# A new order of the engine queues in the gated unit of an S5 layer

## The chip, the cores and the metric

The kernel runs on one core of one Trainium2 chip. A core has five engines with a queue each, worked off strictly in order: TensorE (PE in the profile; its weight loads are PEld), VectorE (DVE), ScalarE (ACT), GpSimd (POOL) and SyncE (SP, which here only issues DMAs). Engines wait for one another through semaphores. The metric is the device time of one execution in microseconds (us), given as the median of several runs.

## The reference, cut to what matters

One layer of a diffusion backbone on 1024 latent tokens of width 1024, with a context prefix of 256 tokens: a bidirectional S5 scan, then a gated unit, then a SwiGLU feed-forward part and a last RMS norm. The part around the change:

```python
g = gelu(y)                                   # y: output of the scan, 1024 x 1024
y = g * sigmoid(g @ w_glu + b_glu)            # the gated unit
x = x + gate * y                              # residual
h = modulate(rms_norm(x, norm_ffn), shift, scale)
x = x + gate2 * ((silu(h @ w1) * (h @ w3)) @ w2)   # 2816 hidden units
return rms_norm(x, norm_final)
```

## The kernel before, in words

Everything is fp32. A matmul operand is split into a high part (a copy rounded to `fp32r`) and a low part (the operand minus its high part), and each product is made of three matmuls, high by high, high by low and low by high.

The 1024 x 1024 x 1024 product `g @ w_glu` is made by a seven-product scheme (`ORDER`, line 1156): seven products of 512 x 512 x 512, whose left operands are blocks, sums and differences of blocks of the weight (L11, L12, S2, S3, L22, S1, S4) and whose right operands are blocks and differences of the activations (R11, R21, T2, T3, T4, T1, R22). The differences T are taken by VectorE, the sums S by DMAs that accumulate.

The order of everything in this unit is written out by hand, as one string of words, `TODO` (line 1157). A loop (`for word in TODO.split(): todo(word)`, line 1371) issues the instructions of one word after the other, so that each engine's queue holds its instructions in the order in which the words stand; the words of different engines are tied only by semaphores. Most words have the form `name:index:...`, and where the engine can be chosen the last letter names it (`D` or `V` VectorE, `P` or `E` GpSimd, `A` ScalarE). The words are (names of `todo`, lines 1232 to 1350):

- `.` or a number: one step, or so many, of TensorE. A step is three matmuls of 128x512 for one k of 4 of one column block q of 4 of one product p: step 16p + 4q + k + 1. Products 0 to 6 are the seven; steps 113 to 128 are the first 16 of the feed-forward part (line 1205). Each block (p, q) gathers in one of five PSUM banks used in rotation, except that product 1 adds into the banks of product 0. So the first step of a block waits until the block five before it has been read for the last time.
- `gT:k:j`, `bT:k:j`: four TensorE transposes (a quad) into one of two further banks; `gA` is the GELU from it (ScalarE), `bC` a copy from it, `bQ` a squared copy from it (ScalarE) and `bR` its sum (VectorE).
- `Rh`, `Rl`, `Wh`, `Wl`: high and low part of a right operand (128x512) or of a half of a left operand (128x1024). The copies are ScalarE's, `Wl` is always GpSimd's, `Rl` is VectorE's (`D`) or GpSimd's (`P`).
- `m`, `t2`, `t3`, `t4`: the differences, on VectorE, from SBUF to SBUF. `s`, `f`, `h`: accumulating DMAs issued from GpSimd's queue (they make S2, S4 and S1). `l`, `x`, `Q`, `R`: loads issued from SyncE's queue (`x:2` the third piece of the residual stream).
- `p` copies a first product's bank to SBUF (ScalarE). `u`, `v`, `c`, `d1`, `d2`, `E1` combine the products' banks (VectorE, one operand in PSUM). Then, for each of the 16 output blocks in the families e, c, d and E, `eS` is the sigmoid (ScalarE), `eM` multiplies by the gate column and by g (VectorE, one operand in PSUM) and `eX` adds the residual. With the letter `s`, `eM` writes to SBUF and frees the bank, and `eX` is GpSimd's; without, `eX` is VectorE's, reads PSUM, and frees the bank.
- `q`: a squared sum (ScalarE). `z:j`: 14 instructions of VectorE, 13 of them 128x4 and nine of those with two SBUF inputs, that make 1/rms of token half j and copy it out to 128x512; `Z:j`: eight TensorE matmuls that spread it over the rows. `hT` (VectorE, one operand in PSUM) applies it; `hH`, or `hI` and `hC`, makes the high part (ScalarE) and `hL` the low part, on VectorE (`V`) or GpSimd (`E`). `hT` writes one of three buffers in rotation.
- `oh`, `ol`: high and low part of the first feed-forward weights (ScalarE, GpSimd). `L:g`, `L:h`, `L:l`: gate, high and low part of the first rows of `w2`. `S:0`, `M:0`, `G:0`: SiLU, product and split of the feed-forward part's first tile.

After the string, `up_plain(0, 1, rest)` (line 1407) goes on with 16 more steps, the matmuls `pu` of the profile, in banks of a new PSUM pool; it needs the first four `hH` and `hL` of token half 1. All later stages are bound to TensorE's queue in the same way.

Two instructions of helpers carry most of the rows: line 78 is every `tensor_tensor`, line 81 every `scalar_tensor_tensor`, on VectorE or GpSimd. In the rows, `pp` are the five rotating banks, `pq` the two banks of the quads, `prb` the bank of `Z`; `c`, `rr`, `ru`, `rxa`, `rxc`, `rw` and `r` lie in SBUF. The step's lines:

```python
if k == 0:
    ZT.append(ZT[q] if p == 1 else pp())
(lh, ll), (rh, rl) = (SL[x] for x in ORDER[p])
cs_, z = slice(P * q, P * q + P), ZT[4 * p + q]
for n, (w, b) in enumerate(((lh, rh), (lh, rl), (ll, rh))):
    PE.matmul(z, w[:, k, cs_], b[:, k], start=p != 1 and k + n == 0, ...)
```

Of the kernel before, what the change touches and what calls it, by code (L numbers as in the profile page):

```python
# [1872 lines left out]
```

## Time and profile before

| | us |
|---|---|
| median of 3 runs | 1033.13 |
| lowest and highest run | 1031.77, 1033.31 |
| the profiled execution's own time | 1031.7 |
| its span | 1029.9 |
| TensorE, VectorE, ScalarE, GpSimd busy over the span | 957.5, 820.9, 450.3, 773.7 |
| the unit, from its first quad (267.35 us) to the first `pu` matmul (390.37 us) | 123.0 |

Start times in the rows are counted from the start of the span. A row of the timeline gives start, duration, engine, line, operation, output<-inputs, shape, how many like instructions are merged in it, and in square brackets the idle time of the engine ahead of it with the instruction that ended it. Neighbouring instructions of one engine overlap in the records by about 0.1 us, so that the cost of one in a row of many is the distance of the starts.

### The profile page before, as it was taken

How to read it: one execution, taken by the hardware profiler on the slowest of the kernel's cores; microseconds unless marked ns; L12 is line 12 of the kernel's file. 1: busy time of each engine (PE TensorE's matmuls, PEld its weight loads, DVE VectorE, ACT ScalarE, POOL GpSimd, SP SyncE). 2: the span in 40 equal slices, each digit the busy share in tenths (PEclk: the TensorE clock that was granted, in tenths of full speed). 3: DMA queues.
4: the chain of work that ended last, by engine and by line, in shares of the span. 5: the costliest groups of instructions: out<-in, count | busy, mean ns of one | idle time of the engine just before them, and what ended most of it. 6: DMA issues, size and time to landing. Idle time of an engine off the chain costs nothing. (4 is left out here: it accounts for less than half of the span.)

```text
span 1029.9 us, 17603 instructions
## 1 busy us (share of the span) xinstructions
PE 957.5 (93%) x6572; PEld 750.8 (73%) x6572; DVE 820.9 (80%) x1580; ACT 450.3 (44%) x827; POOL 773.7 (75%) x595
## 2 busy tenths in 40 slices
PE   5988798878998798999999999999999999999996
PEld 1466523667877676888888888888888888888885
DVE  7979799995589889788877768695968768586977
ACT  4468622323554675534334332434334343424337
POOL 5799899991578355888787777778687877778674
PEclk9989999989999899999999999999999999999998
DMA  9764997213944211011211112121212011121204
GB/s 322 284 136 92 286 349 230 89 52 93 238 102 135 91 42 61 21 41 41 82 42 43 50 46 68 52 71 42 83 41 71 29 55 62 42 72 52 72 21 164
DMA packets 50793, 102.04 MB, mean 99 GB/s; under 512 B 4490, under 2 KB 19082, under 8 KB 49684
## 3 DMA queue, kind: packets, MB, share of 16 engines
q1 hardware_dynamic: 44372, 85.60, 25.2%
q0 software_dynamic: 3168, 11.54, 5.9%
q10 hardware_dynamic: 3168, 3.79, 1.1%
q8 instruction: 52, 0.85, 0.3%
q14 instruction: 33, 0.27, 0.1%
HBM read 85.30 MB, written 6.16 MB: 89 GB/s over the span
## 5 line engine op out<-in xcount | busy, mean ns | idle before, releaser
L78 POOL TENSOR_TENSOR rr<-rxc,rr 128x512 fp32r<-128x512 f32 (+1 forms) x130 | 172.6, 1341 | 63.1 <-ACT rr L1187 56.2
L1358 PE MATMUL ut<-rr,rr 128*128 128x512 f32 x400 | 155.7, 389 | 0.2 <-POOL rr L78 0.2
L1356 PE MATMUL ut<-rr,rr 128*128 128x512 f32 x400 | 155.6, 389 | 0.0
L1187 ACT CAST rr<-rxc 128x512 fp32r<-128x512 f32 x124 | 76.9, 622 | 148.3 <-PE xt L1680 51.5
L1680 PE MATMUL xt<-rr,c 128*128 128x512 f32 x540 | 129.7, 389 | 0.0
L1357 PE MATMUL ut<-c,rr 128*128 128x512 f32 x320 | 124.5, 389 | 0.0
L1680 PEld LDWEIGHTS xt<-rr,c 128*128 128x128 f32 x540 | 101.4, 188 | 21.0
L78 DVE TENSOR_TENSOR ru<-ru,xt 128x1024 f32<-128x1024 f32 x90 | 106.7, 1212 | 8.1 <-PE xt L1680 6.3
L78 DVE TENSOR_TENSOR ru<-ut,ru 128x512 f32<-128x512 f32 x98 | 67.1, 686 | 42.0 <-PE ut L1358 36.5
L1357 PE MATMUL ut<-rr,rr 128*128 128x512 f32 x240 | 93.4, 389 | 0.0
L1358 PEld LDWEIGHTS ut<-rr,rr 128*128 128x128 f32 x400 | 75.1, 188 | 16.3 <-POOL rr L78 0.6
L1356 PEld LDWEIGHTS ut<-rr,rr 128*128 128x128 f32 x400 | 75.1, 188 | 15.6
L1357 PEld LDWEIGHTS ut<-c,rr 128*128 128x128 f32 x320 | 60.1, 188 | 12.4
L78 POOL TENSOR_TENSOR rr<-rw,rr 128x512 fp32r<-128x512 f32 x27 | 37.7, 1396 | 37.8 <-ACT rr L1187 37.8
L78 POOL TENSOR_TENSOR rr<-ru,rr 128x512 fp32r<-128x512 f32 (+1 forms) x40 | 58.7, 1468 | 9.5 <-ACT rr L1187 5.7
L1356 PE MATMUL ut<-c,rr 128*128 128x512 f32 x160 | 62.3, 389 | 0.1
L1358 PE MATMUL ut<-c,rr 128*128 128x512 f32 x160 | 62.2, 389 | 0.0
L78 POOL TENSOR_TENSOR rxc<-rxc 128x512 f32<-128x512 f32 x40 | 60.6, 1516 | 1.6
L1680 PE MATMUL ut<-rr,c 128*128 128x512 f32 x216 | 51.9, 389 | 0.0
L1357 PEld LDWEIGHTS ut<-rr,rr 128*128 128x128 f32 x240 | 45.0, 188 | 9.3
L586 PE MATMUL pv<-ru,c 128*64 128x160 f32 x512 | 45.5, 316 | 5.2 <-ACT ru L499 2.0
L1218 PE MATMUL pp<-rr,rr 128*128 128x512 f32 x192 | 48.1, 407 | 1.9 <-DVE rr L78 1.9
(460 smaller groups left out, 2427.5 us busy)
## 6 DMA issues: line engine op xcount, KB each, us to landing
c<-in_ada_w SPq DMA_DIRECT2D x46, 256.0 KB, 5.5
rxc<-in_w SPq DMA_DIRECT2D x38, 256.0 KB
rxc<-in_w SPq DMA_DIRECT2D x19, 512.0 KB, 3.6
rw<-in_w SPq DMA_DIRECT2D x11, 512.0 KB
ru<-in_w SPq DMA_DIRECT2D x11, 512.0 KB
ra<-in_ada_w SPq DMA_DIRECT2D x10, 512.0 KB, 10.7
ra<-in_ada_w SPq DMA_DIRECT2D x18, 256.0 KB, 6.0
ru<-in_xT SPq DMA_DIRECT2D x4, 1024.0 KB
```

What stands on the lines that cost most here:

```text
L78: eng.tensor_tensor(out=o, in0=x, in1=y, op=op)
L586: PE.matmul(pv[64 * (i % 2):64 * (i % 2) + 64, ri, c0:c0 + 160], w[:, i, 64 * ri:64 * ri + 64], U[:, 8 * b + 4 * j + i], start=True, stop= ...
L1187: S.copy(o[0], x)
L1218: PE.matmul(z, w[:, k, cs_], b[:, k], start=p != 1 and k + n == 0, stop=k == 3 and n == 2, skip_group_check=p == 1)
L1356: PE.matmul(pu, wh, bh, start=start, stop=False)
L1357: PE.matmul(pu, wh, bl, start=False, stop=False)
L1358: PE.matmul(pu, wl, bh, start=False, stop=stop)
L1680: PE.matmul(pd, w[:, cs_], b, start=j in (1, 2, 4) and n == 0, stop=n == 2, skip_group_check=j not in (1, 2, 4))
```

## The change

The string `TODO` is replaced by another. It holds the same work: 128 steps, 26 quads, and the same words, apart from the engine of some: of the `Rl`, R21:2, R22:0, T1:2 and T2:3 go from GpSimd to VectorE and T1:0, T3:2 and T4:3 from VectorE to GpSimd; of the `eM`/`eX` pairs, e:1, e:3, c:0 and E:0 become VectorE's and c:1, c:2, c:3, E:1 and E:3 GpSimd's; of the `hL`, 0:0 and 1:5 go to VectorE and 0:3, 0:5, 1:0 and 1:6 to GpSimd (with `hI` and `hC` in the place of `hH`, or the other way round); of the `bC`, 0:0 and 7:1 go to ScalarE, 0:1, 4:0, 5:1 and 6:0 to VectorE. Otherwise only the order of the words differs, and with it the order of each engine's queue. No other line is changed.

```diff
--- before.py
+++ after.py
@@ -1154,27 +1154,27 @@
 
 
         ORDER = (("L11", "R11"), ("L12", "R21"), ("S2", "T2"), ("S3", "T3"), ("L22", "T4"), ("S1", "T1"), ("S4", "R22"))
-        TODO = """gT:6:0 x:0 . Wh:L12:1 . Rh:R21:0 Wl:L12:1 gT:7:0 Rh:R21:1 . gA:6:0 . gA:7:0 Wh:L12:0 gT:1:1 Rl:R21:0:D s:0 gT:4:1 . Rh:R21:3
-            Rl:R21:1:D gA:4:1 . Wl:L12:0 gA:1:1 . Rh:R21:2 gT:3:1 gT:0:1 gA:3:1 . Rl:R21:3:D s:1 p:0 . m:3 gA:0:1 p:1 . Rl:R21:2:P . t3:0
-            gT:2:1 gT:7:1 m:1 gA:2:1 . m:0 gA:7:1 . m:2 p:2 . t3:3 Rh:T3:0 gT:6:1 t2:0 Wh:S3:0 gT:5:1 Rl:T3:0:D . gA:5:1 t2:3 f:0 . Wh:S2:0
-            t3:1 . t2:1 Rh:T2:3 . Wl:S2:0 p:3 . Rh:T3:1 Rh:T2:0 . gA:6:1 . Rh:T2:1 f:1 Rl:T3:1:D . Wh:S2:1 t3:2 . Rl:T2:3:P Wh:S3:1 2 Rh:T3:2
-            l:0 t2:2 eS:e:0 . Wl:S2:1 2 Rh:T2:2 eM:e:0 . Rh:T3:3 Rl:T2:0:D eS:e:1 . Rl:T2:2:P eX:e:0:D eS:e:2 l:1 . eM:e:1:s . Rl:T2:1:P eM:e:2
-            . eS:e:3 eX:e:2:D bT:0:0 Wh:L22:0 Wl:S3:1 eM:e:3:s 3 Wh:L22:1 . t4:2 Q:2 . u:0 Wl:L22:0 Rh:T4:2 3 Rl:T3:2:D h:0 . Rl:T3:3:D .
-            eX:e:3:P u:1 2 Rl:T4:2:D Wl:S3:0 u:2 . Rh:T1:0 . Rh:T1:1 . Rh:T1:2 bT:2:0 Rh:T1:3 t4:1 . u:3 Rl:T1:2:P Wh:S1:0 2 Rh:T4:1 t4:0 .
-            bC:2:0:A eX:e:1:P Rh:T4:0 . v:0 . Rl:T4:1:D x:1 . Rl:T4:0:P . t4:3 . Wl:L22:1 v:1 . Rh:T4:3 3 Rl:T4:3:D h:1 . Rl:T1:3:D Rh:R22:0
-            x:2 . v:2 Wl:S1:0 Wh:S4:0 . Rh:R22:2 . v:3 Wh:S4:1 . Rl:T1:0:D Q:0 Rh:R22:1 . Rl:R22:0:P bC:0:0:D Rh:R22:3 2 Rl:T1:1:D . c:0
-            Wl:S4:0 Wh:S1:1 bT:1:0 . eS:c:0 bC:1:0:D . eM:c:0:s Rl:R22:3:P . c:1 . eS:c:1 Rl:R22:1:D . Wl:S1:1 eM:c:1 . eX:c:1:D . c:2 . eS:c:2
-            bT:5:0 Wl:S4:1 Q:1 bT:3:0 eM:c:2 bC:5:0:A . bC:3:0:A eX:c:2:D . q:0:0:0 . Rl:R22:2:P c:3 q:0:0:1 R:0 bT:6:0 . eS:c:3 eX:c:0:P
-            q:0:0:2 . eM:c:3 bC:6:0:A . eX:c:3:D q:0:0:3 bT:4:0 L:g x:3 bT:7:0 bC:4:0:A . bC:7:0:A d1:0 . q:1:0:0 d2:0 . q:1:0:1 . eS:d:0 .
-            d1:1 q:1:0:2 . eM:d:0:s q:1:0:3 . d2:1 eX:d:0:P . z:0 eS:d:1 2 oh:0:0 . oh:0:2 ol:0:0 d1:2 bT:4:1 oh:0:3 Z:0 eM:d:1:s bC:4:1:A
-            ol:0:2 d2:2 oh:0:1 . hT:0:0 . eS:d:2 eX:d:1:P d1:3 . hI:0:0 eM:d:2:s hC:0:0 . ol:0:1 hT:0:1 bT:5:1 . d2:3 eX:d:2:P hH:0:1 hT:0:2 .
-            bC:5:1:A eS:d:3 E1:0 . hL:0:0:E hI:0:2 eM:d:3:s bT:6:1 eS:E:0 . hL:0:1:V hC:0:2 . bC:6:1:A eX:d:3:P hT:0:3 . eM:E:0:s hH:0:3 .
-            hL:0:2:E E1:1 . hT:0:4 eS:E:1 eX:E:0:P bT:7:1 hT:0:5 hH:0:4 . bC:7:1:D hH:0:5 . ol:0:3 E1:2 q:1:1:0 . eM:E:1 eS:E:2 . R:1 hL:0:5:V
-            q:1:1:1 bT:0:1 eX:E:1:D L:h . hL:0:3:V . q:1:1:2 eM:E:2 L:l . bC:0:1:A hT:0:6 . q:1:1:3 eX:E:2:D . hI:0:6 E1:3 bQ:0:1 bT:2:1
-            hL:0:4:V hC:0:6 bT:1:1 bR:0:1 eS:E:3 . hL:0:6:E hT:0:7 bC:2:1:A . bQ:1:1 eM:E:3 hI:0:7 bR:1:1 . bC:1:1:A eX:E:3:D bQ:2:1 hC:0:7
-            bR:2:1 bT:3:1 hL:0:7:E bC:3:1:A bQ:3:1 bR:3:1 . z:1 . S:0 3 Z:1 . hT:1:0 . hT:1:2 hH:1:0 . hT:1:1 hH:1:2 . hL:1:0:V hI:1:1 hL:1:2:V
-            hC:1:1 hT:1:3 hL:1:1:E hT:1:5 hH:1:3 M:0 hI:1:5 hL:1:3:V G:0:h hT:1:4 hC:1:5 hT:1:6 hL:1:5:E hH:1:4 hH:1:6 hL:1:4:V hT:1:7 hH:1:7
-            hL:1:6:V hL:1:7:V G:0:l"""
+        TODO = """. x:0 s:0 Rh:R21:0 gT:2:1 Wh:L12:0 gT:4:1 Rl:R21:0:D . gA:4:1 Wl:L12:0 . gA:2:1 . Rh:R21:1 Wh:L12:1 gT:7:1 gT:0:1 . gA:7:1 s:1
+            Rl:R21:1:D gA:0:1 m:2 gT:6:0 p:0 gT:5:1 Wl:L12:1 gA:6:0 . gA:5:1 . Rh:R21:2 . Wh:S2:0 f:0 gT:3:1 m:0 gT:7:0 Rl:R21:2:D . gA:3:1
+            Wl:S2:0 gA:7:0 . Rh:R21:3 . Wh:S2:1 . f:1 . t2:0 p:2 Rl:R21:3:D . Rh:T2:0 Wl:S2:1 . Wh:S3:0 l:0 . gT:1:1 Wh:S3:1 . Wl:S3:0 . p:1
+            p:3 . gA:1:1 . l:1 . Wl:S3:1 3 t3:0 Q:2 . m:1 Rh:T3:0 . t2:1 gT:6:1 m:3 Rh:T2:1 . t2:3 gA:6:1 . Rl:T2:1:P Rh:T2:3 . eS:e:0 . t2:2 .
+            t3:2 . Rh:T2:2 Rl:T2:0:D Wh:L22:0 Rl:T2:3:D . Rl:T2:2:P eM:e:0 . eS:e:3 eX:e:0:D Rh:T3:2 Wl:L22:0 eS:e:1 eM:e:3 . Wh:L22:1 eM:e:1 2
+            eS:e:2 eX:e:1:D . eM:e:2 Wl:L22:1 . eX:e:2:D . u:0 eX:e:3:D . Rl:T3:2:P u:1 . x:1 . h:0 t4:2 bT:3:0 t3:1 . Rh:T4:2 h:1 Rl:T3:0:D
+            Rh:T3:1 . t3:3 . Rh:T1:0 Rl:T3:1:D . Rh:T3:3 u:2 Rl:T1:0:P Rh:T1:1 . Rh:T1:2 . Rl:T1:1:D Rh:T1:3 . Rl:T1:2:D . Rl:T1:3:D t4:0
+            bT:0:0 bC:3:0:A Rl:T4:2:D bC:0:0:A bT:2:0 Rl:T3:3:D Rh:T4:0 bT:1:0 bC:2:0:A u:3 Rl:T4:0:P . Wh:S1:0 bC:1:0:D . v:0 Wh:S1:1 .
+            Wl:S1:0 . q:0:0:0 . q:0:0:1 . v:1 Wl:S1:1 q:0:0:2 Q:0 . q:0:0:3 3 t4:1 Q:1 v:2 . Rh:T4:1 t4:3 Rh:R22:0 . Rl:T4:1:D Rh:T4:3 .
+            Rl:R22:0:D Rh:R22:1 . Rl:T4:3:P v:3 Wh:S4:1 . Rh:R22:2 . Wl:S4:1 x:2 Rh:R22:3 . Wh:S4:0 . c:0 . eS:c:0 Rl:R22:2:P . eM:c:0 .
+            Wl:S4:0 . c:1 . eS:c:1 . eX:c:0:D . Rl:R22:3:P R:0 eM:c:1:s . c:2 eX:c:1:P . eS:c:2 . Rl:R22:1:D . eM:c:2:s . c:3 eX:c:2:P bT:5:0
+            bT:4:0 bC:5:0:A . bC:4:0:D eS:c:3 . eM:c:3:s . L:g 2 eX:c:3:P d1:0 bT:6:0 d2:0 . bC:6:0:D x:3 eS:d:0 . eM:d:0:s bT:7:0 . d1:1
+            eX:d:0:P bC:7:0:A . d2:1 q:1:0:0 . q:1:0:1 . q:1:0:2 . d1:2 q:1:0:3 . d2:2 oh:0:0 . z:0 eS:d:2 . ol:0:0 oh:0:3 . oh:0:2 ol:0:3
+            bT:4:1 oh:0:1 . bC:4:1:A eM:d:2:s . ol:0:1 eS:d:1 d1:3 Z:0 d2:3 eX:d:2:P . hT:0:2 eS:d:3 . eM:d:3:s ol:0:2 hI:0:2 bT:6:1 hT:0:0
+            hC:0:2 . bC:6:1:A eX:d:3:P E1:0 R:1 . hH:0:0 eM:d:1:s . eS:E:0 hL:0:2:E hT:0:1 . E1:1 hH:0:1 bT:7:1 eX:d:1:P hT:0:5 . eS:E:1
+            bC:7:1:A eM:E:0 . hI:0:5 hL:0:0:V . hC:0:5 hT:0:3 bT:5:1 hL:0:5:E . bC:5:1:D hI:0:3 . eM:E:1:s hC:0:3 . q:1:1:0 E1:2 eX:E:1:P .
+            eX:E:0:D eS:E:2 . L:h hL:0:3:E E1:3 bT:0:1 eM:E:2 eS:E:3 bT:1:1 L:l q:1:1:1 hT:0:6 eM:E:3:s q:1:1:2 eX:E:2:D q:1:1:3 bC:0:1:D
+            eX:E:3:P bQ:0:1 hI:0:6 bT:2:1 bR:0:1 hC:0:6 bC:2:1:A hL:0:1:V bQ:1:1 hL:0:6:E hT:0:4 . bC:1:1:A . hH:0:4 bR:1:1 . hL:0:4:V bQ:2:1
+            bT:3:1 . bR:2:1 bC:3:1:A hT:0:7 . bQ:3:1 . hI:0:7 bR:3:1 hC:0:7 z:1 hL:0:7:E . Z:1 S:0 . hT:1:2 . hT:1:0 hH:1:2 . hT:1:1 hI:1:0 .
+            hL:1:2:V hC:1:0 . hI:1:1 hT:1:5 hL:1:0:E . hC:1:1 hH:1:5 . hL:1:1:E hT:1:3 . hH:1:3 hT:1:4 hL:1:3:V hH:1:4 hT:1:6 hL:1:4:V hI:1:6
+            hL:1:5:V hC:1:6 hT:1:7 hL:1:6:E M:0 hH:1:7 G:0:h hL:1:7:V G:0:l"""
         WS = dict(L12=wb, S2=wc, S3=wa, L22=wc, S1=wc, S4=wb)
         XL = ((XA, 0, 0), (XA, 1, 1), (A2, 1, 0), (A2, 0, 1))
         NPL = 2
```

## The prediction

> **What bounds the kernel now.** I read the page first, then the timeline of TensorE over the unit, then the stretches around its gaps, and last VectorE and GpSimd ahead of the longest gap.
>
> ```profile
> PE 957.5 (93%) x6572; PEld 750.8 (73%) x6572; DVE 820.9 (80%) x1580; ACT 450.3 (44%) x827; POOL 773.7 (75%) x595
> ```
>
> TensorE is busy 93% of the span, and the later stages hang on its queue. So the change is worth what it alters of TensorE's idle time between the unit's first quad and the first `pu` matmul.
>
> ```profile
> 267.35 0.60 PE L1246 MATMUL pq<-r,ru 128*128 128x128 f32 x4
> 269.17 1.66 PE L1218 MATMUL pp<-c,c 128*128 128x512 f32 x6 [1.22 <-ACT ru L1007]
> 270.67 0.60 PE L1246 MATMUL pq<-r,ru 128*128 128x128 f32 x4
> ...
> 297.47 1.05 PE L1218 MATMUL pp<-rr,rr 128*128 128x512 f32 x2 [1.87 <-DVE rr L78]
> ...
> 299.02 11.46 PE L1218 MATMUL pp<-rr,rr 128*128 128x512 f32 x45
> 310.32 0.60 PE L1246 MATMUL pq<-r,c 128*128 128x128 f32 x4
> 310.67 11.18 PE L1218 MATMUL pp<-c,c 128*128 128x512 f32 x48
> ...
> 338.33 1.97 PE L1246 MATMUL pq<-r,c 128*128 128x128 f32 x8 [6.50 <-DVE c L78]
> 339.95 3.31 PE L1218 MATMUL pp<-rr,rr 128*128 128x512 f32 x9
> ...
> 356.87 1.16 PE L1150 MATMUL prb<-r,rw 128*128 128x128 f32 x8 [2.28 <-DVE rw L1143]
> ...
> 378.06 0.63 PE L1246 MATMUL pq<-r,rr 128*128 128x128 f32 x4 [0.86 <-ACT ru L1250]
> ...
> 379.85 0.50 PE L1357 MATMUL pp<-rr,rr 128*128 128x512 f32 x1 [0.85 <-POOL rr L78]
> ...
> 383.64 1.16 PE L1150 MATMUL prb<-r,rw 128*128 128x128 f32 x8 [0.33 <-DVE rw L1143]
> ...
> 390.37 0.76 PE L1356 MATMUL pu<-rr,rr 128*128 128x512 f32 x1 [2.82 <-ACT rxa L1324]
> ...
> 402.70 0.39 PE L1356 MATMUL pd<-c 128*128 128x512 f32 x1
> ```
>
> The brackets are TensorE's gaps: 1.22, 1.87, 6.50, 2.28, 0.86, 0.85, 0.33 and 2.82, together 16.7 us of the 123.0 from 267.35 to 390.37. The row of 48 matmuls gives the pace: less the 0.16 by which the last record hangs over, 11.02 us for 16 steps, 0.689 a step. A quad costs 0.35 (310.32 to 310.67) and about 0.1 at the change of shape (six matmuls take 1.50 at 269.17 in place of 1.38): 0.45. A `Z` costs about 1.0.
>
> After a gap TensorE is also slow. The 45 matmuls from 299.02 take 11.30, 1.0 more than at that pace; behind the gap of 6.50 the two quads take 1.62 in place of 0.8, and the nine matmuls 0.35 each, 1.9 more together; the 48 `pu` matmuls take 12.33 (390.37 to 402.70), 1.3 more. The granted clock shows the same:
>
> ```profile
> core 0: us, PE busy (x) PEld busy (x) DVE busy (x) ACT busy (x) POOL busy (x), PEclk, DMA share, GB/s
> 298.00:332.00 34.00, 33.83 (x149) 27.68 (x147) 32.94 (x26) 13.20 (x19) 28.30 (x16) 0.95 0.46 124
> 332.00:338.40 6.40, 0.07 (x1) 0.07 (x2) 6.23 (x9) 1.32 (x2) 6.01 (x4) 0.75 0.65 196
> 387.60:391.00 3.40, 0.63 (x2) 0.56 (x3) 3.40 (x7) 2.76 (x6) 1.27 (x1) 0.83 0.00 0
> ```
>
> Where the gap of 6.50 comes from stands some 15 us earlier:
>
> ```profile
> 316.96 0.67 DVE L78 TENSOR_TENSOR ru<-ru,pp 128x512 f32<-128x512 f32 x1
> ...
> 319.77 8.55 DVE L78 TENSOR_TENSOR rr<-ru,rr 128x512 fp32r<-128x512 f32 x1
> ...
> 337.59 0.69 DVE L78 TENSOR_TENSOR c<-pp,c 128x512 f32<-128x512 f32 x1
> ```
> ```profile
> 316.45 2.85 POOL L78 TENSOR_TENSOR rr<-ru,rr 128x1024 fp32r<-128x1024 f32 x1
> 319.59 0.89 POOL L1049 DMA_DIRECT2D ru<-in_w_glu  x1 [0.30 <-POOL rr L78]
> 320.21 2.73 POOL L78 TENSOR_TENSOR rr<-rxa,rr 128x1024 fp32r<-128x1024 f32 x1
> 322.58 1.60 POOL L78 TENSOR_TENSOR c<-rr,c 128x512 fp32r<-128x512 f32 x1
> 323.83 2.69 POOL L78 TENSOR_TENSOR c<-rxc,c 128x1024 fp32r<-128x1024 f32 x1
> 326.18 1.58 POOL L78 TENSOR_TENSOR c<-rr,c 128x512 fp32r<-128x512 f32 x1
> ```
>
> At 319.77 VectorE has `Rl:T1:0`, with two SBUF inputs. It takes 8.55 us and ends when GpSimd's run of four low parts ends; the like instruction with one input in PSUM takes 0.67 at 316.96, beside a low part of GpSimd. So a two-input instruction of VectorE that meets a GpSimd run waits for all of it. The c family behind it comes 8 us late, and its `eX:c:1` at 337.59 is what the quad `bT:5:0` waited for.
>
> **The change part by part.** TensorE's work stays: 128 steps (88.2), 26 quads (11.7), two `Z` (2.0), 101.9 us. To this come the waits of the new order. I walked through its queues with the durations above (VectorE 0.6 to 0.7 each, GpSimd 1.3 and 2.4, ScalarE as below).
>
> *Start.* The first word is now a step. If its bank is the one for which step 1 waited, TensorE starts at 269.17, 1.8 us after 267.35; if it gets the bank of the old first quad, 0. I take 1.8. From there step 33 comes at 295.7 and step 65 at about 319.7 (before, 310.67 + 11.02 = 321.7).
>
> *Gap of 1.87.* It was a low part of T2 beside GpSimd. GpSimd now does L12, S2 and S3 in one run up to about 288.4; VectorE's `t3:0` waits that run out, and then come nine instructions (5.8 us with their waits for ScalarE) to the low part for step 33: 294.5. The cover is 1.2 us; I cost it 0, bounds 0 and 1.
>
> *Gap of 6.50.* The T1 low parts now stand ahead of step 52, where GpSimd has one low part and then waits; GpSimd's run `Rl:T4:3`, `Wl:S4:1`, `Rl:R22:2`, `Wl:S4:0`, `Rl:R22:3` lies beside v:3, c:0, eM:c:0, c:1 and so on, all with a PSUM operand. The c family then follows TensorE's steps, and `eX:c:1` is done some 1.5 us before `bT:5:0`. Cost 0; without that cover it is rival A. The quads bT:0 to bT:3, moved ahead of steps 44 and 52, need copies finished long before.
>
> ```profile
> 351.29 0.15 DVE L1141 TENSOR_REDUCE r<-r 128x4 f32<-128x8 f32 x1
> 356.39 0.43 DVE L1143 COPY rw<-r 128x512 f32<-128x512 f32 x1
> 380.56 0.17 DVE L1141 TENSOR_REDUCE r<-r 128x4 f32<-128x20 f32 x1
> 383.16 0.43 DVE L1143 COPY rw<-r 128x512 f32<-128x512 f32 x1
> ```
> ```profile
> L1303 ACT ACTIVATE pp<-pp,r 128x512 f32<-128x512 f32 x16 | 10.4, 660 | 13.1 <-DVE pp L78 13.1
> L1310 ACT ACTIVATE ru<-ru 128x512 f32<-128x512 f32 x12 | 7.6, 630 | 0.2
> L1310 ACT ACTIVATION_READ_ACCUMULATOR ru<-ru 128x1 f32 x12 | 2.3, 189 | 0.0
> ```
>
> *Z:0.* The first pair of rows is z:0, 5.5 us beside GpSimd, the second z:1, 3.0 us alone. The new z:0 starts when the fourth `q` is done: 0.6 for `bC:7:0` and four times 0.82, 3.9 after the quad bT:7:0, so near step 95. TensorE has five steps and a quad (3.9) until `Z:0`. Alone, z:0 would cost nothing; but `ol:0:0`, `ol:0:3` and `ol:0:1` (3.9) run beside it, so 3.0 + 3.7 - 3.9 = 2.8. Bounds 0 and 3.
>
> *Step 114.* It needs `hL:0:1`, which stood ahead of step 104 and now stands behind E1:3, eM, hT, eM, eX, bC and bR. E1:3 needs step 112. From there VectorE needs 8 x 0.65 = 5.2; ScalarE needs L:h, eS:E:3, three `q` and `bQ` (1.0 + 0.66 + 2.5 + 0.6 = 4.8) before `bR`, and bR and hL 1.3: 6.1. TensorE has a step and three quads, 2.0. So a new wait of 3.2 to 4.1; I take 4.0.
>
> *Steps 120 and 121.* After `bQ:0:1` ScalarE has eleven instructions (6.6) to `hC:0:7`, then GpSimd's low part (1.3), 7.9; step 114 lies 1.3 behind that `bQ`, and six steps and a quad are 4.6: a wait of 2.0. z:1 ends 10.3 after it, and `Z:1`, which stood ahead of step 125 and now stands ahead of 121, waits 1.7 more. I take 3.5 for both; bounds 2 and 5.
>
> *Tail.* The first `pu` needs hL:1:0 and hL:1:1, which GpSimd has done about 5.6 after `Z:1`; steps 121 to 128 cover 5.5. The gap of 2.82 and its slow 1.3 go, unless rival B holds.
>
> *The DMA queues.* `s:0` now heads GpSimd's queue, ahead of `Wl:L12:0`; it waits only for a sum issued in the stage before, so 0. On SyncE's queue Q:0 and Q:1 go ahead of x:2, which in any case waits for `Rl:T4:3` (321) and is read by `eX:c:0` at about 326; behind that stands the c family with its 1.5 us of cover. No row shows how long such a load takes; I take 0, and 2 as the bound, inside the next item.
>
> *The rest.* For waits that a walk does not see I take 2.0, as much as 0.86 + 0.85 + 0.33 now (bounds 0 and 4), and for the slow clock 1.3, after the wait of 4.0, between 1.0 and 1.9.
>
> **Sum.** 101.9 + 1.8 + 2.8 + 4.0 + 3.5 + 2.0 + 1.3 = 117.3, against 123.0 + 1.3 = 124.3: 7.0 us less. The profiled execution took 1031.7, which gives 1024.7; the median is 1.4 above it, so 1033.1 - 7.0 = 1026.1.
>
> **The rivals.**
>
> *A: VectorE is held up again.* In product 4 `Rl:R22:0`, two inputs in SBUF, is due on VectorE 0.15 us before GpSimd can begin `Rl:T4:3`. If GpSimd is first, at 319.9, it holds through the run of five (three of 1.3, two of 2.4: 8.7); the Rl and v:3 follow, and c:0 begins at 329.8 in place of 322.6, 7.2 late. From there to the end of eX:c:1 are 5.2, while TensorE has 13 steps (9.0) ahead of bT:5:0: a gap of 3.4, and 1.9 of slow clock. That is 1033.1 - 7.0 + 5.3 = 1031.4. For it speaks the row of 8.55, against it the order of readiness. The Trainium skill, "SBUF — State Buffer", section "Who interferes with whom", says that VectorE with two SBUF inputs and GpSimd exclude one another for one instruction, whoever issues first. By that rule VectorE would wait at most one of GpSimd's 2.7 us, rival A would cost nothing, and the time were 1026.1; the trace, with 8.55 through four instructions, does not agree.
>
> ```profile
> 389.55 0.68 DVE L78 TENSOR_TENSOR ru<-pp,ru 128x512 f32<-128x512 f32 x1
> ```
>
> *B: `M:0` gates the first `pu`.* Now `pu` begins 0.14 after M:0 ends (390.23), as if it took over the bank that M:0 reads. M:0 was the eighth VectorE instruction after `Z:1` and is now the 13th, behind two that wait for GpSimd: 10.3 after Z:1, less 5.5 of steps, a gap of 4.8 and 1.3 slow: 1032.2. Against it: banks are handed out in the order of first use, which now begins with a step, and the string could then be free of that tie.
>
> ```profile
> rxc<-rxa POOLq DMA_DIRECT2D x1, 512.0 KB, 5.4
> ru<-in_w_glu POOLq DMA_DIRECT2D x1, 512.0 KB, 8.8
> ```
>
> *C, the slower side: late weights.* `h:0` and `h:1` now follow each other at about 302.7, beside the load x:1. `Wh:S1:1` waits for h:1, and behind it on ScalarE stand four `q`, `Rh:T4:1` and what feeds step 66 (5.7 us, due at 320.6), so h:1 may land at 314.9 for nothing. One after the other, 8.8 each, it lands at 320.3, with a load of such length ahead at 329; halfway, 324.7, TensorE stands 9.8 and is slow 1.9 more: 1033.1 - 7.0 + 11.7 = 1037.8. It decides from a landing at about 320, where the gain is gone. Against it: f:0 landed in 5.4 though it was issued while another was on its way.
>
> *D: the gain is eaten.* If the waits at Z:0 and step 114 are twice mine, 6.8 more: 1032.9, no change.
>
> **How the numbers follow.** About 0.2%, 2.1 us, is what a measurement of this kernel can tell from no change. My forecast has 0.62 (0.57 faster, 0.04 same, 0.01 slower), A 0.12 (0.04, 0.06, 0.02), B 0.10 (0.05, 0.04, 0.01), C 0.08 (slower), D 0.08 (0.06 same, 0.02 slower). Together faster 0.66, same 0.20, slower 0.14. The range goes down to 1021.5, where the start costs nothing and the 2.0 and part of Z:0 fall away, and up to 1032.5, over A and B; C, D and the outer ends are left out.
>
> **What would show it.** Right: no row of VectorE above 5 us between 300 and 330, no gap ahead of bT:5:0, step 65 near 319.7, a gap of 2 to 3 us ahead of Z:0 and of about 4 ahead of step 114, first `pu` near 382 to 385. Wrong: a VectorE row of 8 us beside the run in product 4 (A), `pu` starting right behind M:0 (B), ScalarE idle for a DMA into `ru` (C), or waits beyond 6 us at Z:0 and step 114 (D).

## The result and the profile after

The kernel after takes 1027.44 us (median of 9 runs, 1022.8 to 1029.48), the kernel before beside it 1031.83 us (9 runs, 1029.89 to 1037.39). The ratio, estimated over all the runs (that of the two medians is 0.9957), is 0.9944, with a 95% interval from 0.9921 to 0.9967: faster by 0.3 to 0.8%. The profiled execution of after took 1025.44 us, with a span of 1023.7.

The busy times, then TensorE's rows in the unit that answer to those shown of before; a bracket is the idle time ahead of the row and what ended it.

```profile
PE 956.7 (93%) x6572; PEld 750.1 (73%) x6572; DVE 808.0 (79%) x1580; ACT 450.8 (44%) x827; POOL 774.1 (76%) x597
```
```profile
267.85 0.93 PE L1218 MATMUL pp<-c,c 128*128 128x512 f32 x3
269.26 1.09 PE L1246 MATMUL pq<-r,ru 128*128 128x128 f32 x8 [0.47 <-ACT ru L1007]
...
320.15 11.73 PE L1218 MATMUL pp<-rr,rr 128*128 128x512 f32 x51
...
348.65 1.16 PE L1150 MATMUL prb<-r,rw 128*128 128x128 f32 x8 [2.17 <-DVE rw L1143]
...
365.47 1.12 PE L1246 MATMUL pq<-r,rr 128*128 128x128 f32 x4 [3.80 <-ACT ru L1250]
...
373.92 0.50 PE L1356 MATMUL pp<-rr,rr 128*128 128x512 f32 x1 [0.26 <-ACT rr L1326]
...
375.26 0.50 PE L1357 MATMUL pp<-rr,rr 128*128 128x512 f32 x1 [0.84 <-POOL rr L78]
...
377.54 1.35 PE L1150 MATMUL prb<-r,rw 128*128 128x128 f32 x8 [1.54 <-DVE rw L1143]
...
385.60 0.39 PE L1356 MATMUL pu<-rr,rr 128*128 128x512 f32 x1
```

TensorE's work is the same; its idle time in the unit is not. The gaps of 6.50 (ahead of bT:5:0), 1.87 (product 2) and 2.82 (ahead of `pu`) are gone. A gap of 3.80 is new, and the one ahead of `Z:1` grew from 0.33 to 1.54. Together 9.1 us are left of 16.7. From the first quad or step to the first `pu` it is now 117.75 us (267.85 to 385.60) where it was 123.0. From there to the end of the span it is 638.1, where it was 639.5. The stages ahead of the unit ended 0.5 us later in this execution (267.85 against 267.35). 5.3 + 1.4 - 0.5 = 6.2 is the difference of the spans (1029.9 - 1023.7).

The granted clock tells the rest (columns: stretch, its length, busy time and count of each engine, granted clock, DMA share, GB/s):

```profile
core 0: us, PE busy (x) PEld busy (x) DVE busy (x) ACT busy (x) POOL busy (x), PEclk, DMA share, GB/s
332.00:338.40 6.40, 6.40 (x37) 5.41 (x36) 5.60 (x9) 1.81 (x3) 3.34 (x3) 1.00 0.10 22
360.00:372.00 12.00, 8.20 (x32) 6.48 (x31) 9.03 (x14) 9.04 (x18) 6.62 (x5) 0.72 0.00 1
378.00:386.00 8.00, 8.00 (x33) 6.61 (x32) 5.67 (x9) 5.31 (x8) 2.58 (x2) 0.79 0.00 0
```

Where before had its gap of 6.50 the clock is now 1.00, not 0.75. But it is 0.72 around the new gap of 3.80 and 0.79 behind `Z:1`.

VectorE still has one long row, in product 1, beside three low parts of GpSimd. Note the DMA issue at 281.46, ahead of the three; the experiments come back to it.

```profile
278.56 0.68 DVE L78 TENSOR_TENSOR c<-rr,ru 128x512 f32<-128x512 f32 x1
280.49 1.69 DVE L78 TENSOR_TENSOR rr<-c,rr 128x512 fp32r<-128x512 f32 x1 [1.25 <-ACT rr L1258]
282.11 8.04 DVE L78 TENSOR_TENSOR ru<-rr 128x512 f32<-128x512 f32 x1
```
```profile
278.30 0.88 POOL L1277 DMA_DIRECT2D rxc<-rxa  x1 [1.42 <-DMA rxa<-rxa]
278.92 2.71 POOL L78 TENSOR_TENSOR rr<-rxa,rr 128x1024 fp32r<-128x1024 f32 x1
281.46 1.00 POOL L1277 DMA_DIRECT2D rxc<-ru  x1
282.07 2.82 POOL L78 TENSOR_TENSOR rr<-ru,rr 128x1024 fp32r<-128x1024 f32 x1
284.45 2.80 POOL L78 TENSOR_TENSOR c<-rxa,c 128x1024 fp32r<-128x1024 f32 x1
286.81 2.78 POOL L78 TENSOR_TENSOR c<-rw,c 128x1024 fp32r<-128x1024 f32 x1
```

The row of 0.68 is `t2:0`, that of 1.69 `Rl:R21:3`, that of 8.04 `t3:0`. TensorE does not wait for `t3:0`.

### The profile page after: what moved, and what is told of

Its sections match the earlier page's. It is cut to its first block, busy times and chain, and to the rows that moved or that the text cites. A ratio compares the mean times of both kernels' runs of the same rounds, so it can differ in the third digit from the quotient of the medians.

```text
span 1023.7 us, 17603 instructions
## 1 busy us (share of the span) xinstructions
PE 956.7 (93%) x6572; PEld 750.1 (73%) x6572; DVE 808.0 (79%) x1580; ACT 450.8 (44%) x827; POOL 774.1 (76%) x597
## 5 line engine op out<-in xcount | busy, mean ns | idle before, releaser
L78 POOL TENSOR_TENSOR rr<-r,rr 128x512 fp32r<-128x512 f32 x25 | 32.3, 1291 | 21.2 <-ACT rr L1187 19.3
```

The source lines that it names most:

```text
L78: eng.tensor_tensor(out=o, in0=x, in1=y, op=op)
```

## Experiments

Twelve kernels were run, each a few words of the string away from before or after. "The unit" below is the time from the first step to the first `pu` in the profile: 121.20 us before (269.17 to 390.37), 117.75 after. In orders that begin with a quad, as before does, 1.82 us more lie ahead of the first step.

**What held VectorE in product 4 of before.** First, two of the low parts that the change moves were moved alone.

```diff
--- before
-. v:3 Wh:S4:1 . Rl:T1:0:D Q:0 Rh:R22:1 .
-Rh:R22:3 2 Rl:T1:1:D . c:0
+. v:3 Wh:S4:1 . Q:0 Rh:R22:1 .
+Rh:R22:3 2 . c:0
-. u:3 Rl:T1:2:P
+. u:3 Rl:T1:0:D Rl:T1:1:D Rl:T1:2:P
```

> The order of before, with two words moved: the low parts T1:0 and T1:1 go on VectorE's queue from product 4, where GpSimd's run of four stood, to behind u:3 in product 3. Theory (the 6.50 us gap and its slow clock came from VectorE held up by that run): no VectorE row above 5 us between 315 and 335, the gap ahead of bT:5:0 under 1.5, the time 5 to 8 us under before. Rival 1 (the gain of the change came from its first and last words, that is from which banks come first): no change, within 2 us of before. Rival 2 (a wait is only moved to the next two-input instruction): a VectorE row of 4 us or more elsewhere in product 4 and less than 3 us gained.

Measured: 1031.57 us (12 runs) against 1032.36, ratio 0.9989 (0.9978 to 1.0), where 5 to 8 us less were expected. The long row stayed:

```profile
319.53 8.55 DVE L78 TENSOR_TENSOR rr<-ru,rr 128x512 fp32r<-128x512 f32 x1
```

It could not be `Rl:T1:0`, which now stood elsewhere. In the order of the words the first low part there is `Rl:T1:3`; the prediction named the wrong word. The gap only fell from 6.50 to 5.41. So all three were moved:

```diff
--- before, with the edit above
-. Rl:T1:3:D Rh:R22:0
+. Rh:R22:0
-. u:3 Rl:T1:0:D Rl:T1:1:D Rl:T1:2:P
+. u:3 Rl:T1:3:D Rl:T1:0:D Rl:T1:1:D Rl:T1:2:P
```

> The kernel before, with three of VectorE's low parts, Rl:T1:3, Rl:T1:0 and Rl:T1:1, moved from product 4 to behind u:3, so that VectorE reads no finished SBUF pair while GpSimd's four instructions of product 4 run. The row of 8.55 us at 319.53 in the order before is Rl:T1:3, the first of the three (the earlier run moved only the other two and left it standing). Theory (VectorE held behind a run of GpSimd keeps c:0 and the evictions behind it late, and the products' PSUM banks with them): no VectorE row over 3 us between 315 and 335, the gap of 6.50 us ahead of the quad of product 4 goes down to at most 1, and the time falls by 4 to 8 us against before, to some 1024 to 1028. Rival one (another VectorE instruction takes the wait in product 4, R22:0 or R22:1): a row of 5 to 8 us stands there under another name and the gap stays at 4 to 6, time within 2 us of before. Rival two (the gap is given back at u and Z, where the chain of element work ends last anyway): gap gone, gaps ahead of Z:0 or pu grow by as much, time within 2 us.

Measured: 1030.15 (9 runs) against 1032.02, ratio 0.9968 (0.9951 to 0.9985); the unit is 118.50.

```profile
335.99 1.90 PE L1246 MATMUL pq<-r,c 128*128 128x128 f32 x8 [3.75 <-DVE c L78]
```

No VectorE row over 2.2 us is left in product 4, and the 2.75 that the gap lost arrived whole at `pu` (387.87 - 269.37 against 121.20: 2.70 less). That settles that the held row cost time on the path. But 3.75 of the gap stays, and the gain was less than the 4 to 8 us expected. What stays ends on ScalarE:

```profile
330.50 1.05 ACT L1261 CAST rr<-ru 128x1024 fp32r<-128x1024 f32 x1 [6.21 <-DMA ru<-in_w_glu]
```

`Wh:S1:1` stands ahead of the first sigmoid of the c family and waits 6.21 us for the load `h:1`. In before that wait was 4.50:

```profile
328.43 1.05 ACT L1261 CAST rr<-ru 128x1024 fp32r<-128x1024 f32 x1 [4.50 <-DMA ru<-in_w_glu]
```

It was over at 328.43, 0.1 us behind the end of the held row; a second cause stood ready behind the first. Part of the 3.75 the edit made itself, though: GpSimd issues `h:1` at 321.78 here and at 319.59 in before, 2.0 us later counted from the first step. How much of the gap the load alone would have kept in before is not shown.

**Was `Rl:R22:0` a near miss in after?** It began 0.2 us ahead of GpSimd's run (rival A). It was put later, first by one place, then into the run.

```diff
--- after
-Rl:R22:0:D Rh:R22:1 . Rl:T4:3:P v:3 Wh:S4:1
+Rh:R22:1 . Rl:T4:3:P v:3 Rl:R22:0:D Wh:S4:1
```

> The order after, with one word moved by one place: Rl:R22:0 on VectorE stands behind v:3 in place of ahead of it, so that GpSimd begins its run of low parts first. Theory (a two-input VectorE instruction waits for a whole run of GpSimd): a VectorE row of 7 to 10 us, a gap of 2 to 5 us ahead of bT:5:0 or bT:4:0, and 3 to 6 us above the order after, so 0 to 3 us under before. Rival (it waits for one instruction of GpSimd at most): a row of 1 to 3 us, no gap ahead of bT:5:0, and the time of the order after, about 5.8 under before.

```diff
--- after
-Rl:R22:0:D Rh:R22:1 . Rl:T4:3:P
+Rh:R22:1 . Rl:T4:3:P
-. c:0 . eS:c:0
+. c:0 Rl:R22:0:D . eS:c:0
```

> The kernel after, with VectorE's low part Rl:R22:0, which in the profile began 0.2 us before GpSimd's run of product 4 (320.05 against 320.26), put behind c:0, inside that run, so that it cannot win. Theory (a two-operand SBUF instruction of VectorE is held until GpSimd's back-to-back instructions end): a row of 5 to 9 us at about 321.3 to 324, ending at 327.8 or at 330.4, a gap of 2 to 5 us on TensorE ahead of bT:5:0 or of the quad of product 4, and the time 2 to 5 us above after. Rival (it waits for one instruction of GpSimd only, 2.40 us at most, as the Trainium skill has it): a row of at most 3.1 us, no gap on TensorE, time within 1 us of after.

Measured: 1026.51 (6 runs, ratio 0.994, 0.992 to 0.996) and 1026.32 (6 runs, 0.9937, 0.992 to 0.9954), so neither differs from after. In the second, VectorE and GpSimd did this:

```profile
327.05 0.76 DVE L78 TENSOR_TENSOR c<-rr,c 128x512 fp32r<-128x512 f32 x1
```
```profile
324.85 2.40 POOL L78 TENSOR_TENSOR c<-rxc,c 128x1024 fp32r<-128x1024 f32 x1 [0.18 <-ACT c L1261]
327.22 1.74 POOL L78 TENSOR_TENSOR c<-rr,c 128x512 fp32r<-128x512 f32 x1
```

`Rl:R22:0` came between two low parts of a run and went first; GpSimd's next took 1.74 in place of 1.3. So a run as such does not shut VectorE out, and my theory behind rival A fell.

The first of the two showed something else, though, far from the edit: in product 1 the row of `Rl:R21:3` (1.69 in after) had become the held one.

```profile
280.94 7.97 DVE L78 TENSOR_TENSOR rr<-c,rr 128x512 fp32r<-128x512 f32 x1
```
```profile
288.97 6.44 PE L1218 MATMUL pp<-rr,rr 128*128 128x512 f32 x20 [2.94 <-DVE rr L78]
```

`Rl:R21:3` feeds TensorE, `t3:0` does not yet. Of the six profiles with after's words unchanged in products 0 and 1, two show the row of 8 us at `t3:0` (after, and a run below with `ol` later), three show it at `Rl:R21:3` with gaps of 2.94, 3.18 and 3.00, and one shows no such row and a gap of 0.61. In the first two of the three, whose tail is that of after, the unit is 121.99 and 121.62 instead of 117.75. The same order thus has outcomes some 4 us apart.

**Can the tie be taken out?** `Rl:R21:3` was put ahead of `t2:0`.

```diff
--- after
-f:1 . t2:0 p:2 Rl:R21:3:D . Rh:T2:0
+f:1 . Rl:R21:3:D p:2 t2:0 . Rh:T2:0
```

> The kernel after, with VectorE's low part Rl:R21:3 one place earlier, ahead of t2:0, so that it reaches its SBUF operands before GpSimd's run Wl:S2:1, Wl:S3:0, Wl:S3:1 can begin. Theory (whether VectorE or GpSimd comes first there is decided by some 0.1 us and differs from execution to execution; lost, Rl:R21:3 waits 7.97 us and the gap of 2.94 us appears, as in the run of R22:0 one place later, whose profile put pu at 389.40 and not 385.60): every execution now wins, so the times lie closer together than the after order's 1022.8 to 1029.5 (within some 3 us), and the median falls by 2 to 4 us against after, to 1023 to 1025. Rival (the spread has another cause, such as the clock or the transfers in later stages): spread as wide as after's, median within 1 us of after.

Measured: 1025.97 (6 runs, 1024.68 to 1028.13), ratio 0.9934 (0.9917 to 0.995). The spread is narrower, 3.5 over six runs against 6.7 over nine, but the median fell by less than the 2 to 4 expected, within the intervals. `Rl:R21:3` was held in the profile all the same (4.95 us at 279.66), with a gap of 1.82 on TensorE (behind a copy on ScalarE that stood behind `Rh:T2:0`, and so behind the held row). The edit is no cure.

**What makes it long: the DMA issue.** Looking again through all profiles, each VectorE instruction that waited for more than one GpSimd instruction had met a DMA issue in GpSimd's queue: 319.59 before (row of 8.55), 281.46 after (row of 8.04, above). Not every one that met an issue waited: `t2:0` of after, above, began 0.26 us into the issue of 278.30, ahead of the low part at 278.92, and took 0.68. Two kernels test it. In before, the issue `h:1` was taken from ahead of the run; the run and `Rl:T1:3` stay. Far from it, `M:0` was put earlier, to see what `pu` waits for.

```diff
--- before
-Rl:T4:3:D h:1 . Rl:T1:3:D
+Rl:T4:3:D . Rl:T1:3:D
-Wl:S4:0 Wh:S1:1 bT:1:0
+Wl:S4:0 h:1 bT:1:0
-Rl:R22:1:D . Wl:S1:1 eM:c:1
+Rl:R22:1:D . Wh:S1:1 Wl:S1:1 eM:c:1
-hT:1:3 hL:1:1:E hT:1:5 hH:1:3 M:0 hI:1:5
+M:0 hT:1:3 hL:1:1:E hT:1:5 hH:1:3 hI:1:5
```

> The kernel before with two edits far apart. First, GpSimd's DMA issue h:1 is taken from ahead of its run of product 4 (issue 319.59, run 320.21 to 327.76) and put behind the third instruction of the run, with ScalarE's Wh:S1:1, which reads what it loads, put later as well; the run itself and VectorE's Rl:T1:3 stay. In every profile so far, each VectorE instruction that waited through more than one GpSimd instruction (3.9 to 8.6 us) had met a GpSimd DMA issue; beside runs without one (the run of z:0 after, the run of product 4 after with R22:0 inside) none waited longer than one instruction. Theory one (the DMA issue is what makes VectorE lose the whole run): the row of Rl:T1:3 falls from 8.55 to at most 3.0 us. Theory two (any run of ready GpSimd instructions holds it until the queue is empty): the row stays at 6 to 9 us. Second edit: VectorE's M:0 stands ahead of hT:1:3 and hT:1:5. In the order before, the first matmul on pu waits for VectorE and ScalarE, and M:0 ended at 390.23 where pu began at 390.37; in the order after, that matmul waits for no VectorE instruction. If M:0 sets pu there: pu starts 1.2 to 1.4 us earlier against the matmul ahead of it, the gap of 2.82 us becomes 1.4 to 1.6. If it was another instruction: the gap stays at 2.8. Time: 1 to 4 us under before by theory one, within 2 us of it by theory two, less the 1.3 us of M:0; the later load may cost some of it ahead of product 5.

```profile
319.27 2.90 DVE L78 TENSOR_TENSOR rr<-ru,rr 128x512 fp32r<-128x512 f32 x1
...
323.29 0.68 DVE L78 TENSOR_TENSOR rr<-ru,rr 128x512 fp32r<-128x512 f32 x1
```
```profile
318.76 2.86 POOL L78 TENSOR_TENSOR rr<-rxa,rr 128x1024 fp32r<-128x1024 f32 x1
321.58 1.75 POOL L78 TENSOR_TENSOR c<-rr,c 128x512 fp32r<-128x512 f32 x1
323.30 2.92 POOL L78 TENSOR_TENSOR c<-rxc,c 128x1024 fp32r<-128x1024 f32 x1
```
```profile
331.73 1.09 PE L1246 MATMUL pq<-r,c 128*128 128x128 f32 x8 [0.37 <-DVE c L78]
...
340.50 1.09 PE L1246 MATMUL pq<-r,c 128*128 128x128 f32 x8 [2.38 <-POOL c L78]
...
386.58 0.47 PE L1356 MATMUL pu<-rr,rr 128*128 128x512 f32 x1 [1.51 <-DVE ru L78]
```

`Rl:T1:3` meets the same low parts and waits for one of them, 2.90 in place of 8.55; the next of its kind, at 323.29, goes between GpSimd's second and third. The gap of 6.50 ahead of bT:5:0 becomes 0.37, and at the next quads stand 0.51 and 2.38 (GpSimd's low part there now waits for the later load; and `Wh:S1:1` no longer stands ahead of the first sigmoid). `pu` waits 1.51 in place of 2.82 and is let go by `M:0`, which was put 1.3 us earlier: `M:0` did set it in before. Measured: 1028.74 (12 runs) against 1032.6, ratio 0.9961 (0.9944 to 0.9977); the unit is 118.04, with both edits in it. Theory one holds for this row.

The other kernel took a DMA issue from between the four low parts of product 1 in after and put it ahead of them.

```diff
--- after
-Wl:S2:0 gA:7:0 . Rh:R21:3 . Wh:S2:1 . f:1 . t2:0
+f:1 Wl:S2:0 gA:7:0 . Rh:R21:3 . Wh:S2:1 . . t2:0
```

> The kernel after with GpSimd's accumulating DMA issue f:1 put ahead of Wl:S2:0, right behind f:0, so that no DMA issue stands between GpSimd's four low parts Wl:S2:0, Wl:S2:1, Wl:S3:0 and Wl:S3:1. VectorE's Rl:R21:3 comes to them at about 280.5, in the middle of the first. Theory one (the DMA issue makes VectorE lose the whole run): Rl:R21:3 and t3:0 wait for at most one GpSimd instruction each, rows of 1 to 3 us instead of the 8.04 us at 282.11, no gap over 0.5 us on TensorE in products 0 and 1, the spread of the times narrows, and the time is 0 to 3 us under after. Theory two (any run of ready instructions holds VectorE to its end): one row of 6 to 8 us stays, at Rl:R21:3 or at t3:0, with the gap of some 3 us on TensorE where it is Rl:R21:3.

```profile
280.07 10.57 DVE L78 TENSOR_TENSOR ru<-rr 128x512 f32<-128x512 f32 x1
```
```profile
279.74 0.86 POOL L1277 DMA_DIRECT2D rxc<-ru  x1 [1.60 <-DMA ru<-rw]
280.30 2.73 POOL L78 TENSOR_TENSOR rr<-rxa,rr 128x1024 fp32r<-128x1024 f32 x1
...
287.37 2.71 POOL L78 TENSOR_TENSOR c<-rw,c 128x1024 fp32r<-128x1024 f32 x1
```

Read by its numbers alone, this was not what theory one expected: a row of 10.57 stood there. But the premise had failed. `f:1` now waited 1.60 us for another DMA, so that the four began only at 280.30, and `t3:0` arrived at 280.07, during the issue. It then lost to all four. The edit thus made the condition that it was to remove, and one more low part behind it made the row longer, 10.57 in place of 8.04. Measured: 1027.09 (6 runs), ratio 0.9951 (0.9932 to 0.9971), no change; this time `Rl:R21:3` went ahead free, and TensorE's gap was 1.72, in product 2.

**Start and bank order.** The quad was put ahead of the first step again, as in before.

```diff
--- after
-""". x:0 s:0 Rh:R21:0 gT:2:1
+"""gT:2:1 . x:0 s:0 Rh:R21:0
```

> The order after, with one word moved: the quad gT:2:1 stands ahead of the first step, so that the banks are handed out in the order of before. Theory (banks go by first use, and so M:0 does not hold up pu in the order after): TensorE starts its first step about 1.3 us later, behind both copies of ScalarE, and the first pu matmul begins 0.1 to 0.2 us after M:0 ends, with a gap of 3 to 5 us ahead of it; 4 to 6 us above the order after, 0 to 2 under before. Rival (the pu wait of before had another cause): no gap ahead of pu, and the time of the order after, about 5.8 under before.

Measured: 1023.79 (6 runs), ratio 0.9917 (0.99 to 0.9935). The first step waits 1.22 again, as in before, where in after it waits for nothing and the quad behind it 0.47: whichever comes second waits. But `pu`, at 384.88, does not wait, and `M:0` is at 388.06. So in after's order `M:0` does not gate `pu`, whatever comes first; rival B's premise does not carry over, though it was right for before, and that the string begins with a step is not what frees it. The interval overlaps that of after (0.9921 to 0.9967).

**The gap ahead of `Z:0`.** `z:0` takes 6.1 us beside a run of three low parts. They were put later.

```diff
--- after
-. ol:0:0 oh:0:3 . oh:0:2 ol:0:3
+. oh:0:3 . oh:0:2
-eM:d:2:s . ol:0:1 eS:d:1
+eM:d:2:s . eS:d:1
-E1:0 R:1 . hH:0:0
+E1:0 . hH:0:0
-eX:d:1:P hT:0:5 . eS:E:1
+eX:d:1:P ol:0:0 hT:0:5 . eS:E:1
-hL:0:6:E hT:0:4 . bC:1:1:A
+hL:0:6:E ol:0:1 ol:0:3 R:1 hT:0:4 . bC:1:1:A
```

> The order after, with GpSimd's low parts ol:0:0, ol:0:3 and ol:0:1 (and the load R:1, which must follow them) moved from beside z:0 to places where GpSimd was idle later. Theory (z:0 is stretched by them, and its wait is on the path): z:0 takes about 3.0 us in place of 6.0, the gap ahead of Z:0 goes from 2.2 to under 0.5, and the time is 2 to 4 us under the order after. Rival (the tail hangs on a chain of ScalarE and VectorE that does not begin with z:0): the gap goes, and comes back ahead of step 114 or of Z:1; no change against the order after, within 1.5 us.

A row of `z:0` and GpSimd beside it, in after:

```profile
345.33 1.21 DVE L78 TENSOR_TENSOR r<-r 128x4 f32<-128x4 f32 x1
```
```profile
342.74 3.78 POOL L78 TENSOR_TENSOR rr<-rxc,rr 128x512 fp32r<-128x512 f32 x3 [3.27 <-ACT rr L1266]
```

and the same row with the low parts away:

```profile
342.94 0.17 DVE L78 TENSOR_TENSOR r<-r 128x4 f32<-128x4 f32 x1
```

This instruction of 0.17 us waited for a low part of 1.26, and two more of `z:0` did the same. Without them the gap ahead of `Z:0` is gone, the unit is 115.29, and the median is 1022.59 (6 runs, 1019.43 to 1024.28), ratio 0.9902 (0.9882 to 0.9923).

**The wait of 3.80 at bT:2:1.** Three steps were put ahead of it. In this kernel the first of them uses the low part `hL:0:1` before it has been made.

```diff
--- after
-hI:0:6 bT:2:1
+hI:0:6 . . . bT:2:1
-hL:0:6:E hT:0:4 . bC:1:1:A . hH:0:4 bR:1:1 . hL:0:4:V
+hL:0:6:E hT:0:4 bC:1:1:A hH:0:4 bR:1:1 hL:0:4:V
```

> The kernel after, with the three steps 114 to 116 of the last product put ahead of the transposes bT:2:1, where TensorE waits 3.80 us for ScalarE's copy bQ:0:1 and then runs them at the half clock, 0.43 us per matmul. Theory one (the wait and the clock that it costs are on the path): the wait falls to about 1.8 us, some 9 matmuls run at 0.23 instead of 0.43, and the time falls by 2 to 4 us. Theory two (the tail hangs on ScalarE and VectorE, from bQ over bR to z:1, and TensorE waits for them in any case): the gaps ahead of Z:1 grow by what is saved, first pu within 0.7 us of 385.60, time within 1 us of after.

Measured: 1024.67 (6 runs, 1022.25 to 1028.78), ratio 0.9918 (0.9896 to 0.994). The wait split, 1.75 ahead of bT:2:1 and 2.11 ahead of the next quad: 3.86, as much as the 3.80. So the time without work does not go. The nine matmuls put ahead ran at 0.23 each and not at 0.43; six behind the second quad still ran at half clock (375.37 to 378.45, 3.1 us for 1.4 of work), and none did behind `Z:1`. So the slow clock of the tail fell from 4.6 us in after to 1.7. From `Z:0` to `pu` it took 33.5 us, where after's tail took 35.4 to 37.0 in six profiles. Neither theory was quite right: the wait is not on TensorE's side to remove, but the half clock is worth some 2 to 3 us. That a kernel which waits for `hL:0:1` keeps this is not shown. Another try had the copies before that quad earlier:

```diff
--- after with ol later
-bT:0:1 eM:E:2 eS:E:3 bT:1:1 L:l q:1:1:1
+bT:0:1 eM:E:2 bC:0:1:D eS:E:3 bT:1:1 L:l bQ:0:1 q:1:1:1
-q:1:1:3 bC:0:1:D eX:E:3:P bQ:0:1 hI:0:6
+q:1:1:3 eX:E:3:P hI:0:6
```

> The kernel after with the low parts ol:0:0, ol:0:1, ol:0:3 and R:1 put later, as in the run that took the gap ahead of Z:0 away (1022.59 us), and now also with VectorE's copy bC:0:1 directly behind eM:E:2 and ScalarE's bQ:0:1 ahead of q:1:1:1. In the profile after, bT:2:1 waits 3.80 us for bQ:0:1, which stands behind three squares (361.96 to 364.2) and 0.63 us for bC:0:1, while its transposes were done at about 361.0. Theory one (this wait is on the path): the wait at bT:2:1 falls from 3.7 to under 1.5 us, TensorE runs less at the half clock behind it, pu starts 2 to 4 us earlier in the unit and the time is 2 to 4 us under 1022.6. Theory two (the end of the unit hangs on the chain bR, z:1, Z:1 on ScalarE and VectorE): the wait falls, the waits at steps 120, 121 and ahead of Z:1 grow by as much, and the time is within 1 us of 1022.6.

Measured: 1022.61 (6 runs), ratio 0.9907 (0.9885 to 0.9929).

```profile
361.83 0.88 PE L1246 MATMUL pq<-r,rr 128*128 128x128 f32 x4 [2.53 <-DVE rr L78]
364.16 0.79 PE L1357 MATMUL pp<-rr,rr 128*128 128x512 f32 x1 [1.03 <-DVE rr L81]
```

In place of 3.70 for the squares there now stand 2.53 for `eX:E:2`, which makes what is transposed, and 1.03 for `hL:0:1`, together 3.56. Theory two had the time right, but not the place: the waits at steps 120 and 121 and ahead of `Z:1` did not grow (0.26, 0.84 and 1.53). Both waits now end on VectorE, so what is late in the tail is its chain of element work.

**All that pointed the right way.** `ol` later, the quad first, and `f:1` put behind `Wl:S3:0`, where VectorE should want no pair from SBUF.

```diff
--- after, with the edits of ol later and quad first
-. Wh:S2:1 . f:1 . t2:0
+. Wh:S2:1 . . t2:0
-Wh:S3:1 . Wl:S3:0 . p:1
+Wh:S3:1 . Wl:S3:0 f:1 . p:1
```

> The kernel after with what the runs so far point to: ol:0:0, ol:0:1, ol:0:3 and R:1 later (no gap ahead of Z:0), the quad gT:2:1 ahead of the first step (pu 0.7 us earlier in that run), and GpSimd's DMA issue f:1 taken out of the run Wl:S2:1, Wl:S3:0 and put behind Wl:S3:0, where VectorE waits for ScalarE and wants no SBUF pair. Theory one (the DMA issue makes VectorE lose the run: 8.55 us with it and 2.90 without it in the order before, 10.57 us with it ahead of four low parts): Rl:R21:3 and t3:0 wait for one GpSimd instruction each, rows of at most 3.1 us in products 0 and 1, no gap of 1.8 to 3.2 us on TensorE there in any execution, first step to pu in 113.5 to 115.5 us, median 1019 to 1021.5, spread under 4 us. Theory two (the spread and the gap in products 0 and 1 have another cause): a row of 5 to 8 us stays there, median 1021.5 to 1023.

```profile
278.01 2.89 DVE L78 TENSOR_TENSOR c<-rr,ru 128x512 f32<-128x512 f32 x1
...
283.65 2.89 DVE L78 TENSOR_TENSOR ru<-rr 128x512 f32<-128x512 f32 x1
286.46 3.31 DVE L78 TENSOR_TENSOR ru<-rr,c 128x512 f32<-128x512 f32 x1
```
```profile
277.49 2.86 POOL L78 TENSOR_TENSOR rr<-rxa,rr 128x1024 fp32r<-128x1024 f32 x1
...
283.14 2.85 POOL L78 TENSOR_TENSOR c<-rxa,c 128x1024 fp32r<-128x1024 f32 x1
285.93 0.87 POOL L1277 DMA_DIRECT2D rxc<-ru  x1
286.55 2.67 POOL L78 TENSOR_TENSOR c<-rw,c 128x1024 fp32r<-128x1024 f32 x1
```

The row of 8 us has become four of about 2.9, one VectorE instruction after each low part; only the last, which met the DMA issue, took 3.31, a little over the 3.1 expected. No gap is left in products 0 and 1 but the 1.22 ahead of the first step. The unit is 112.88, and with the 1.82 ahead of it 114.70, against 115.29 with `ol` later alone. The median is 1021.27 (6 runs, 1019.57 to 1024.51), ratio 0.99 (0.9875 to 0.9925): faster than before by some 1%. Its interval hardly touches after's (0.9921 to 0.9967); against after with `ol` later alone (1022.59) the runs do not decide. The spread stayed at 4.9 us, where under 4 was expected, so not all of it comes from the held row.

## Why the prediction was right, and where its terms were off

**The sum.** 1026.1 was predicted and 1027.44 measured; 117.3 us for the unit, and 117.75 in the profile. The saving was put at 7.0; the profiled spans differ by 6.2 and the medians by 4.4: the 1033.13 from which the forecast started came out as 1031.83 beside after. With the term for the work left at 101.9, the waits were given as 12.1 (1.8, 2.8, 4.0 and 3.5) and measured 9.1, and to the two small terms, 2.0 and 1.3, fall the other 6.8. So the near hit owes something to errors of opposite sign. The first `pu`, at 385.60, came just behind the 382 to 385 named as a sign.

**Start.** 1.8 was taken and 0 came, the bound below: the first step did not get the bank for which it had waited. By step 65 this was spent. From the first step it took 52.3 us (267.85 to 320.15), where the walk had 50.5.

**Gap of 1.87.** It was costed at 0 because `t3:0` would wait the run out and nobody waits for `t3:0`. That is what the profiled execution shows. But the step failed in taking that order as certain: in three of six profiles `Rl:R21:3` is caught in its place, for 2.9 to 3.2 us of gap and some 4 us in the unit. That the median of after lies 2.0 above its own profiled execution fits; that the longer executions lost their time this way was not shown.

**Gap of 6.50.** Cost 0, and so it was: no VectorE row over 2.9 us between 300 and 330, no gap ahead of bT:5:0. The mechanism named was half right. VectorE was held, by the run and by a first instruction that was `Rl:T1:3` and not `Rl:T1:0`, and with the three low parts moved the gap lost 2.75 of its 6.50. Behind it stood ScalarE's wait for `h:1`, which the prediction had not seen; its own share in before is open, since that edit also delayed the load. In after that load is issued at 303.96, 15.6 us sooner, and both causes are gone. That any such instruction "waits for all of it" was seen only where a DMA issue of GpSimd was met, and not always there.

**Z:0, step 114, steps 120 and 121.** 2.8, 4.0 and 3.5 predicted; 2.17, 3.80 and 2.64 (0.26 + 0.84 + 1.54) measured. The first cause is shown by the run that put the low parts later; its sum took 3.7 for low parts that it had put at 3.9, and they held `z:0` for 3.1 (6.1 against 3.0 without them). The second is named too narrowly: the quad bT:2:1 waited, ahead of the step, and what the runs show behind the wait is VectorE's chain as a whole.

**The slow clock** was the term most mis-sized, 1.3. From 365.47 to 371.63 TensorE does work of 3.2 us and takes 6.2, and from 378.55 to 381.96 work of 1.8 and takes 3.4: 4.6 us in these two places. I had let only the longest gap cost clock; the second place stands behind gaps of 0.84 and 1.54 close together (see the last section).

**Tail.** The gap ahead of `pu` and 1.4 us behind it went as said. `M:0` was the cause in before, as rival B supposed, and is none in after.

**Rivals.** A: `Rl:R22:0` won its tie, and would have lost nothing when put into the run. The Trainium skill ("SBUF — State Buffer", section "Who interferes with whom") says that the one who issues first has the shared ports for that instruction and the other waits. The trace agrees where no DMA issue is near (2.90 us beside a low part of 2.86); where one was met it does not (8.55 through four, 10.57 through four). The prediction had weighed this rule against a single row and drew too much from the row. C: `h:1` landed in 10.3 us, at 314.2; ScalarE waited 1.43 for it and TensorE not at all; up to 314.9 the prediction had it cost nothing. D did not come: no wait was beyond 4 us.
